# A two-layer encoder in one kernel: which engine forms the seven-product sums of the down-projection's weights, when a table slot is freed, and where four square sums and the norm factor stand

## The chip, the cores and the metric

The kernel runs on one core of one Trainium2 chip. The metric is the time of one execution in device microseconds (us), as the median of several executions. The core's engines each have their own list of instructions and run it in order: TensorE (PE in the profile; PEld is its weight load), VectorE (DVE), ScalarE (ACT), GpSimd (POOL), and SyncE (SP), whose list here holds nearly all loads from HBM.

## The reference, cut to what matters

One sequence of 512 tokens with 1024 features passes two layers, all in fp32. Each layer is an attention block and then an MLP; the change touches only the two MLPs.

```python
def rmsnorm(x, g):
    y = xf * lax.rsqrt(jnp.mean(xf * xf, axis=-1, keepdims=True) + EPS)
    return y * g

def sq_relu_mlp(h, w_up, w_down):          # w_up (1024, 4096), w_down (4096, 1024)
    u = jax.nn.relu(h @ w_up)
    return (u * u) @ w_down

for layer in range(2):
    ...
    h = h + sq_relu_mlp(rmsnorm(h, norm_ffn[layer]), ffn_w_up[layer], ffn_w_down[layer])
return rmsnorm(h, final_norm)
```

Below, `h @ w_up` is the MLP's first product and `(u * u) @ w_down` its second. "MLP0" and "MLP1" are the MLPs of the first and the second layer (`mlp(0)` and `mlp(1, last)` in the code).

## The kernel before

**Precision.** Every fp32 operand is split into a high part, which ScalarE rounds (`ACT.activation(hi, raw, Copy)`), and a low part, which VectorE forms as the rest (`raw - hi`). A product is then three matmuls: high by high, high by low, low by high. They are L607 to L609 with 512 columns, and L451 to L453 with 256 columns in the scheme below. The residual stream `hT` stays on the chip, transposed, in eight tiles of 128 by 512.

**Memory.** There are 32 slots of 128 x 1024 fp32 (`Slot`, `NSLOT`); `free` lists those not in use. Beside them stand rings: `raw` (four buffers for weights as loaded), `whi` (three) and `wlo` (four) for their parts.

**The seven-product scheme.** Most of both MLP products go through the class `Seven`: a block of 256 by 256 weights times two blocks of activations needs seven products of half-size blocks instead of eight, at the cost of sums of weight blocks before and sums of results after. One *chunk* is such a block of weights. `seven_chunk` makes one in three steps:

1. a load of 256 KB on SP into a `raw` buffer, or into a slot if more than `reserve[0]` slots are free;
2. three sums of weight blocks, L357, L358 and L359, on the engine `eng` (GpSimd when none is given);
3. the high part on ScalarE (L363), the low part on VectorE (L364). They write rings; a slot used for the raw weights is then given back.

`Seven.run` runs a *group*: a loop over the chunks (`kp`), and in it seven products (L451 to L453). At its end follows the evacuation: L459 on ScalarE, L460 to L463 on VectorE, and then `evac`, which in the second product of an MLP adds the result to `hT` on VectorE (L1579).

**Order of the weights.** `plan` lists the chunks in the order in which they will be used, and `weights(i)` runs ahead of use: the load is issued five chunks ahead (LOAD), and the sums directly with it in program order; high and low parts come two chunks ahead (AHEAD). Each engine's list is then what the scheduler of the framework makes of the program; what is wrapped in `keep_in_program_order` is fixed. `seven_chunk` fixes its sums on GpSimd, and lets the scheduler place sums on VectorE.

**The second product of an MLP** (`mlp`). `stage` computes the squared activations in two shares, and a first part of the second product runs between and after them. Then come four groups `m` = 0 to 3 of 256 output columns each, of eight chunks in MLP0 and seven in MLP1 (`SIZES`). During the groups, `beside(m, i)` is called at each product `i`; in MLP0 it splits the two halves of a last pair of raw activations, `V`, into high and low parts (`split`, L964), at `m == 1`. A short remaining product (`gens4`) uses them after the groups. Ahead of the groups, `reserve[0]` is 3.

**The table slot.** `bias_rows` builds the second layer's position-bias table in a slot `F`, and writes it out to HBM piece by piece by DMA; it runs in MLP0 beside the product ahead of the groups. The slot is kept as `hold["tables"]` and given back after the four groups.

**The planned engine.** `Seven.plan` gives VectorE the sums of chunk `kp == 3` (the fourth) in groups two to four (`c0` above 0, `pairs` given, that is only in the second products); all other chunks' sums are GpSimd's.

**The front of an MLP** (`first_product`). Eight tiles of `hT` are split (`split_g`), and their squares are formed on ScalarE (L621) and summed into `acc` (`sumsq_acc`, L623), all sums on VectorE. Matrix products on values not yet normalised begin at once (`plain`). Between two of them, `norm` computes the norm's factor: `compact_r` sums over partitions with TensorE (L628) and takes the inverse root with some small VectorE operations (L630, then L180 to L190); `bcast_cols` spreads it by four transposes on TensorE (L636), and ScalarE copies it to `rb` (L1368), which the evacuations of these products need. In MLP0 all this is called at product 11, in MLP1 at 13.

Of the kernel before, what the change touches and what calls it, by code (L numbers as in the profile page):

```python
# [30 lines left out]
def f32(ap):  # L31
    return ap.bitcast(F32)
# [3 lines left out]
def encoder_kernel(ctx: ExitStack, tc: tile.TileContext, ins, out, dbg=None):  # L36
    nc = tc.nc
    PE, ACT, DVE, POOL, SP = nc.tensor, nc.scalar, nc.vector, nc.gpsimd, nc.sync
# [37 lines left out]
    def bank(tag, bufs):  # L76
        return ps.tile([P, 512], F32, tag=tag, bufs=bufs, name=nm(tag))
# [4 lines left out]
    def sbk():  # L82
        return bank("s", 2)

    def stb():
        return bank("t", 2)

    def ob():
        return bank("o", 1)
# [180 lines left out]
    def plan(*spec, make=None):  # L270
        asked.append((make or chunk, spec))
        return len(asked) - 1
# [72 lines left out]
    reserve = [3]  # L345
# [23 lines left out]
    class Seven:  # L369
# [62 lines left out]

        def plan(self, w, c0, pairs=None):

            return [plan(w, pairs[kp] if pairs else 2 * kp, c0, DVE if pairs and c0 and kp == 3 else None,
                         make=seven_chunk)
                    for kp in range(self.np)]

# [131 lines left out]
    def tiles(c0, n):  # L570
        return [(c0 + o, min(P, n - o)) for o in range(0, n, P)]
# [46 lines left out]
    def sumsq_acc(k, acc, eng=None):  # L618

        sq = acc if k == 0 else scratch()  # L620
        ACT.activation(sq, hT[:, k, :], AF.Square)  # L621
        if k:
            (eng or POOL).tensor_tensor(acc, acc, sq, op=ALU.add)  # L623

    def compact_r(acc):
        b = stb()
        for i in range(4):
            PE.matmul(b[:, i : i + 1], acc[:, i * P : (i + 1) * P], ones[:, 0:1], start=True, stop=True)  # L628
        v = tiny(4)
        DVE.tensor_scalar(v, b[:, 0:4], 1.0 / D, EPS, op0=ALU.mult, op1=ALU.add)  # L630
        return rsqrt(v, 4)
# [8 lines left out]
    acc = pp.tile([P, S], F32, tag="p", name=nm("acc"))  # L640
# [150 lines left out]
    hold = {}  # L791
# [550 lines left out]
    def first_product(l):  # L1342

        w = ins["ffn_w_up"][l]
        X = [Slot() for _ in range(KD)]
        acc = pp.tile([P, S], F32, tag="p", name=nm("acc"))
        for k in range(KD):
            split_g(hT[:, k, :], gffn(l, k), X[k].pair())
            sumsq_acc(k, acc, DVE)
        xp = [s_.pair() for s_ in X]  # L1350
        U, R = [], []
        rb = keep([P, S], F32, "rb")
        state = dict(c=SIZES[l][0], ids=None, plain=False, split=iter(()), late=iter(()))
        x7 = Seven(KD)

        def ev(j, b):
            U.append(Slot())
            t = scratch()
            DVE.scalar_tensor_tensor(t, b, 0.0, rb, op0=ALU.max, op1=ALU.mult)
            uu = scratch()  # L1360
            ACT.activation(uu, t, AF.Square)
            split(uu, U[-1].pair())

        def norm():
            r = compact_r(acc)
            bk = stb()
            bcast_cols(lambda i: r[:, i : i + 1].to_broadcast([P, P]), P, bk)
            ACT.activation(rb, bk, AF.Copy)  # L1368

        def x_sums(kp):  # L1370
            raw = Slot(F32)
            for z in range(2):
                k = 2 * kp + z
                DVE.scalar_tensor_tensor(raw.t[:, S * z : S * z + S], hT[:, k, :], gffn(l, k), rb, op0=ALU.mult,
                                         op1=ALU.mult)
            for _ in x7.sums(kp, raw):
                pass

        held = tc.keep_in_program_order

        def finish(w_, to):

            held(ACT.activation(w_.t, w_.t, AF.Relu))
            held(ACT.activation(w_.t, w_.t, AF.Square))
            yield
            if to:
                for z, u in enumerate(to):
                    src, d = w_.t[:, S * z : S * z + S], u.pair()
                    held(ACT.activation(d[:, 0, :], src, AF.Copy))
                    held(DVE.tensor_tensor(d[:, 1, :], src, f32(d[:, 0, :]), op=ALU.subtract))  # L1390
                    if z == 0:
                        yield
                w_.free()
            yield

        def raw_evac(w_):
            R.append(w_)
            state["late"] = finish(w_, None)
            return True

        def pair_evac(w_):
            to = []
            for _ in range(2):

                left = state["n"] - len(U)
                to.append(Slot() if left > 3 or not state["halves"] else Halves(spare_p if left < 3 else spare_b))
                U.append(to[-1])
            state["late"] = finish(w_, to)
            return True

        def plain():
            four = product(w, 0, xp, tiles(0, 512), ev, lambda n: [mmb(), mmb(), mmb(), sbk()])
            two = product(w, 0, xp, tiles(512, 256), ev, lambda n: [sbk(), ob()], kstep=4)
            for n, _ in enumerate(four):
                if n == (11 if l == 0 else 13):
                    norm()
                if n == 14:
                    x_sums(0)
                    x_sums(1)
            for n, _ in enumerate(two):  # L1420
                if n == 4:
                    x_sums(2)
                if n == 6:
                    x_sums(3)
            flip[0] = 1
            for s_ in X:
                s_.free()
            state["plain"] = True

        def later(c, n):  # L1430

            for _ in state["split"] if (c, n) in ((0, 10), (0, 18), (1, 4)) else ():
                pass
            if (c, n) in ((0, 2), (0, 10), (0, 18), (1, 4)):
                state["split"] = x7.split({(0, 2): 0, (0, 10): 1, (0, 18): 2, (1, 4): 3}[c, n], tc.keep_in_program_order)
            next(state["split"], None)

        def ahead():
            state["ids"] = x7.plan(w, P * state["c"])

        def stage(n, raw=0, more=0):


            at = [], []
            if not state["plain"]:
                plain()
                at[0].extend(range(0, n, 2))
            nu, nr = (n - len(U)) // 2, raw // 2
            state["n"], state["halves"] = n, raw

            kinds = [1, 0] * nu if nr else [0] * nu
            kinds += [1] * (nr + nu - len(kinds)) + [1] * (more // 2)
            for i, kind in enumerate(kinds):
                ids = state["ids"]
                if i < nu + nr:
                    at[kind].append(state["c"])
                state["c"] += 2
                if i < len(kinds) - 1:
                    ahead()
                for u, _ in enumerate(x7.run(ids, (pair_evac, raw_evac)[kind])):  # L1460
                    if u in (14, 21, 24):
                        next(state["late"], None)
            if state["c"] == 32:
                x7.free()
            got = U[:n], R[: raw // 2], R[raw // 2 :], at, state["late"]
            U.clear()
            R.clear()
            return got

        return stage, ahead, later  # L1470
# [39 lines left out]
    def mlp(l, last=None):  # L1510
# [6 lines left out]
        w = ins["ffn_w_down"][l]  # L1517
        up4, gens4 = [], []

        def plain_last(k0, V):  # L1520
            left = list(V)
            gens4.extend(product(w, k0, up4, tiles(512 * c, 512), lambda j, b, c=c: ev(4 * c + j, b), nk=2 * len(V))
                         for c in range(2))

            def beside(m, i):
                if m == 1 and i % 8 == 4 and left:
                    w_ = left.pop(0)
                    for z in range(2):
                        U4.append(Slot())
                        up4.append(U4[-1].pair())  # L1530
                        split(w_.t[:, S * z : S * z + S], up4[-1])
                    w_.free()

            return beside
# [36 lines left out]
        for x in (work, bias):  # L1571
            for _ in x:
                pass
        reserve[0] = 3
        for m in range(4):

            def evac(w_):
                h2 = hT[:, 2 * m : 2 * m + 2, :]
                DVE.tensor_tensor(h2, h2, w_.t.rearrange("p (z n) -> p z n", z=2), op=ALU.add)  # L1579

            for i, _ in enumerate(u7.run(ids[m], evac)):
                beside(m, i)
        u7.free()
        if not last:
            hold["tables"].free()
        for gen in gens4:
            for _ in gen:
                pass
# [7 lines left out]
    acc = pp.tile([P, S], F32, tag="p", name=nm("acc"))  # L1596
# [481 lines left out]
```

## Time and profile before

| | before |
|---|---|
| median of three runs | 1160.11 us (1159.15 to 1160.34) |
| the profiled execution: its own time | 1159.6 us |
| the profiled execution: its span | 1157.8 us, mean granted clock 0.998 |
| ScalarE busy | 668.3 us (58%) |
| GpSimd busy | 591.3 us (51%) |
| moved by DMA | 134.37 MB, mean 116 GB/s |
| read from HBM | 110.61 MB |

The first row is the median over plain executions; the profile is of one further execution, so durations in the trace stand against that one's time. The span runs from the first instruction to the last. A "wait" in a view is idle time of an engine just ahead of an instruction, with the instruction on another engine, or the DMA, that ended it; "total, times, longest" stand behind it. In a timeline, a row has the start, the duration, the engine, the line, the operation, output and input by the names in the program, and in square brackets the idle time before it. Windows give, for a stretch of time, its length and then the busy time (with the number of instructions) of TensorE, its weight loads, VectorE, ScalarE and GpSimd in this order; the granted clock, the DMA share and GB/s follow.

The four groups of MLP0's second product begin at 494.42, 514.18, 534.20 and 555.53 us of the span, those of MLP1's at 1054.04, 1071.30, 1088.58 and 1106.85.

### The profile page before, as it was taken

How to read it: one execution, taken by the hardware profiler on the slowest of the kernel's cores; microseconds unless marked ns; L12 is line 12 of the kernel's file. 1: busy time of each engine (PE TensorE's matmuls, PEld its weight loads, DVE VectorE, ACT ScalarE, POOL GpSimd, SP SyncE). 2: the span in 40 equal slices, each digit the busy share in tenths (PEclk: the TensorE clock that was granted, in tenths of full speed). 3: DMA queues.
4: the chain of work that ended last, by engine and by line, in shares of the span. 5: the costliest groups of instructions: out<-in, count | busy, mean ns of one | idle time of the engine just before them, and what ended most of it. 6: DMA issues, size and time to landing. Idle time of an engine off the chain costs nothing.

```text
span 1157.8 us, 20539 instructions
## 1 busy us (share of the span) xinstructions
PE 1145.4 (99%) x7348; PEld 1022.4 (88%) x7348; DVE 896.9 (77%) x1562; ACT 668.3 (58%) x1135; POOL 591.3 (51%) x725
## 2 busy tenths in 40 slices
PE   9999999999999999999999999999999999999997
PEld 7787888888899999899988998988889999989995
DVE  6887988878867777967785666667996788697775
ACT  6676877755346668533354555545553666773445
POOL 4356252207688992378602232231387799436850
PEclk9999999999999999999999999999999999999999
DMA  7322414222523336923536574433344233372332
GB/s 236 105 75 70 99 55 137 65 67 97 167 81 98 86 92 157 257 92 101 157 98 164 144 180 128 117 108 119 103 152 127 74 92 92 79 188 71 119 119 73
DMA packets 115351, 134.37 MB, mean 116 GB/s; under 512 B 9796, under 2 KB 96753, under 8 KB 115249
## 3 DMA queue, kind: packets, MB, share of 16 engines
q1 hardware_dynamic: 110896, 120.09, 35.1%
q0 software_dynamic: 4032, 12.60, 5.4%
q8 instruction: 58, 0.95, 0.4%
q10 hardware_dynamic: 320, 0.36, 0.1%
q14 instruction: 45, 0.36, 0.1%
HBM read 110.61 MB, written 6.29 MB: 101 GB/s over the span
## 4 chain that ended last, share of the span: by engine, by line
PE 91%; DVE 3%; POOL 2%; DMA 1%; issue 1%; ACT 0%; DVEq 0%; POOLq 0%; ACTq 0%
PE mm L607 9%; PE mm L609 9%; PE mm L608 9%; PE mm L453 4%; PE mm L451 4%; PE mm L452 4%; PE s L1131 3%; PE t L451 3%; PE t L453 3%; PE t L452 3%; PE o L1119 3%; PE s L609 2%; PE s L608 2%; PE s L607 2%; PE t L1106 2%; PE s L451 2%
## 5 line engine op out<-in xcount | busy, mean ns | idle before, releaser
L607 PE MATMUL mm<-a,whi 128*128 128x512 f32 x428 | 173.6, 406 | 0.2
L364 DVE TENSOR_TENSOR wlo<-a,whi 128x896 fp32r<-128x896 f32 x103 | 126.1, 1227 | 57.5 <-ACT whi L363 56.8
L609 PE MATMUL mm<-a,wlo 128*128 128x512 f32 x428 | 169.0, 396 | 0.0
L608 PE MATMUL mm<-a,whi 128*128 128x512 f32 x428 | 168.9, 395 | 0.0
L363 ACT ACTIVATE whi<-a 128x896 fp32r<-128x896 f32 x103 | 97.8, 949 | 108.1 <-PE s L452 24.4
L233 ACT ACTIVATE whi<-raw 128x1024 fp32r<-128x1024 f32 (+3 forms) x100 | 92.2, 924 | 68.4 <-PE s L608 24.4
L223 DVE TENSOR_TENSOR wlo<-raw,whi 128x1024 fp32r<-128x1024 f32 (+4 forms) x97 | 110.0, 1139 | 26.7 <-ACT whi L233 26.4
L453 PE MATMUL mm<-a,wlo 128*128 128x256 f32 x430 | 120.7, 281 | 0.2
L451 PE MATMUL mm<-a,whi 128*128 128x256 f32 x430 | 120.7, 281 | 0.0
L452 PE MATMUL mm<-a,whi 128*128 128x256 f32 x430 | 120.3, 280 | 0.0
L363 ACT ACTIVATE whi<-raw 128x896 fp32r<-128x896 f32 x61 | 57.7, 952 | 84.4 <-POOL raw L359 44.6
L364 DVE TENSOR_TENSOR wlo<-raw,whi 128x896 fp32r<-128x896 f32 x61 | 73.7, 1222 | 35.9 <-ACT whi L363 35.8
L359 POOL TENSOR_TENSOR a<-a 128x128 f32<-128x128 f32 x103 | 95.3, 926 | 8.1
L358 POOL TENSOR_TENSOR a<-a 128x256 f32<-128x256 f32 x103 | 93.1, 904 | 8.1
L609 PEld LDWEIGHTS mm<-a,wlo 128*128 128x128 f32 x428 | 80.3, 188 | 18.1
L607 PEld LDWEIGHTS mm<-a,whi 128*128 128x128 f32 x428 | 80.5, 188 | 17.2 <-issue 0.8
L608 PEld LDWEIGHTS mm<-a,whi 128*128 128x128 f32 x428 | 80.7, 189 | 14.9 <-DVE a L964 0.2
L1139 POOL TENSOR_SCALAR p<-p,ti 128x512 f32<-128x512 f32 x64 | 45.2, 707 | 85.9 <-DVE ti L1138 61.3
L1721 POOL TENSOR_SCALAR p<-p,ti 128x256 f32<-128x256 f32 x64 | 35.3, 563 | 104.5 <-DVE ti L1720 91.4
L451 PE MATMUL t<-a,whi 128*128 128x256 f32 x312 | 87.6, 281 | 0.0
L453 PE MATMUL t<-a,wlo 128*128 128x256 f32 x312 | 87.3, 280 | 0.0
L452 PE MATMUL t<-a,whi 128*128 128x256 f32 x312 | 87.3, 280 | 0.0
(432 smaller groups left out, 3587.9 us busy)
## 6 DMA issues: line engine op xcount, KB each, us to landing
a<-in_ffn_w_up_dram SPq DMA_DIRECT2D x102, 256.0 KB, 2.8
raw<-in_ffn_w_down_dram SPq DMA_DIRECT2D x34, 512.0 KB, 4.5
raw<-in_ffn_w_down_dram SPq DMA_DIRECT2D x59, 256.0 KB, 2.7
raw<-in_od_w_qkv_dram SPq DMA_DIRECT2D x64, 128.0 KB, 3.0
raw<-in_ffn_w_up_dram SPq DMA_DIRECT2D x12, 512.0 KB, 3.9
wlo<-in_ffn_w_down_dram POOLq DMA_DIRECT2D x12, 512.0 KB, 6.3
a<-a SPq DMA_DIRECT2D x18, 256.0 KB, 3.3
bx<-a SPq DMA_DIRECT2D x32, 128.0 KB, 5.4
```

The lines of the kernel that those rows point to most:

```text
L223: z = lambda: (eng or DVE).tensor_tensor(to, src, f32(high), op=ALU.subtract)
L233: ACT.activation(hi[:, 0:m], raw[:, 0:m], AF.Copy)
L358: held(eng.tensor_tensor(r[:, 4:6], r[:, 2:3].to_broadcast([P, 2, P]), r[:, 0:7:6], op=ALU.add))
L359: held(eng.tensor_tensor(r[:, 7], r[:, 3], r[:, 5], op=ALU.subtract))
L363: ACT.activation(hi[:, 0:896], raw[:, 128:1024], AF.Copy)
L364: DVE.tensor_tensor(lo[:, 0:896], raw[:, 128:1024], f32(hi[:, 0:896]), op=ALU.subtract)
L451: PE.matmul(o, wh, x[:, 0], start=kp == 0 and n in (0, 1, 3, 5), stop=False, skip_group_check=True)
L452: PE.matmul(o, wh, x[:, 1], start=False, stop=False, skip_group_check=True)
L453: PE.matmul(o, wl, x[:, 0], start=False, stop=kp == self.np - 1, skip_group_check=True)
L607: PE.matmul(o, wh, xh, start=first, stop=False)
L608: PE.matmul(o, wh, xl, start=False, stop=False)
L609: PE.matmul(o, wl, xh, start=False, stop=last)
```

## The change

It has five parts:

- *Sums:* in groups two to four of both second products, the chunks `kp` 2 and 5 (the third and the sixth) have their sums on VectorE, in place of chunk 3 (the fourth).
- *Slots:* in MLP0, the table slot is given back before the second group (`m == 1`) and not after the fourth, and `reserve[0]` is 2 during the groups. So more raw weights may be loaded into slots in place of `raw` buffers. MLP1 keeps 3, and has no table.
- *Split of the last raw pair* (`beside`): in MLP0 at `m == 2` instead of `m == 1`.
- *Square sums:* in MLP0, the sums of squares of tiles 1 to 4 go to GpSimd; tiles 5 to 7, and all of MLP1, stay on VectorE. Tile 0 has none.
- *Norm:* `norm` becomes a generator of two steps. In MLP0 the factor is computed at product 8 and spread at product 12 (both were at 11); in MLP1 both stay at 13.

```diff
@@ Seven.plan
-            return [plan(w, pairs[kp] if pairs else 2 * kp, c0, DVE if pairs and c0 and kp == 3 else None,
+            return [plan(w, pairs[kp] if pairs else 2 * kp, c0, DVE if pairs and c0 and kp in (2, 5) else None,
                          make=seven_chunk)
                     for kp in range(self.np)]
@@ first_product
         for k in range(KD):
             split_g(hT[:, k, :], gffn(l, k), X[k].pair())
-            sumsq_acc(k, acc, DVE)
+            sumsq_acc(k, acc, DVE if l or k > 4 else POOL)
...
         def norm():
             r = compact_r(acc)
+            yield
             bk = stb()
             bcast_cols(lambda i: r[:, i : i + 1].to_broadcast([P, P]), P, bk)
             ACT.activation(rb, bk, AF.Copy)
+            yield
...
+            factor = norm()
             for n, _ in enumerate(four):
-                if n == (11 if l == 0 else 13):
-                    norm()
+                for _ in range(((8, 12), (13, 13))[l].count(n)):
+                    next(factor)
@@ mlp, beside
-                if m == 1 and i % 8 == 4 and left:
+                if m == 2 and i % 8 == 4 and left:
@@ mlp
-        reserve[0] = 3
+        reserve[0] = 3 if last else 2
         for m in range(4):
+            if m == 1 and not last:
+                hold["tables"].free()
...
             for i, _ in enumerate(u7.run(ids[m], evac)):
                 beside(m, i)
         u7.free()
-        if not last:
-            hold["tables"].free()
```

## Prediction

> **What bounds the kernel now.** First the page's head, then the waits of the matrix engine's weight loader, which stands ahead of each matmul and so shows a late operand first.
>
> ```profile
> span 1157.8 us, 20539 instructions
> PE 1145.4 (99%) x7348; PEld 1022.4 (88%) x7348; DVE 896.9 (77%) x1562; ACT 668.3 (58%) x1135; POOL 591.3 (51%) x725
> ...
> PEld s L453 <- DVE wlo L364: 1.4, 1, 1.4
> ...
> PEld mm L453 <- DVE wlo L364: 0.8, 3, 0.3
> ...
> PEld t L636 <- DVE ti L190: 0.7, 1, 0.7
> ```
>
> TensorE has something to do for 99% of the span, and the change takes no matmul away. So it can only gain what TensorE waits for. The waits are "total, times, longest". L453 is the third matmul of a product of Seven.run, the one that needs the low weight part made at L364. It waits 1.4 us once and 0.8 us in three further cases, 2.2 us in all. L636, the broadcast of the first MLP's norm factor, waits 0.7 us. These two places are what the change can reach.
>
> The timelines of TensorE and VectorE show the large wait. Chunks of a group are counted from one; eight make a group in the first MLP.
>
> ```profile
> 534.20 0.28 PE L451 MATMUL s<-a,whi 128*128 128x256 f32 x1
> ...
> 541.65 0.28 PE L451 MATMUL s<-a,whi 128*128 128x256 f32 x1
> 541.77 0.28 PE L452 MATMUL s<-a,whi 128*128 128x256 f32 x1
> 543.29 0.38 PE L453 MATMUL s<-a,wlo 128*128 128x256 f32 x1 [1.24 <-DVE wlo L364]
> ```
>
> ```profile
> 532.79 1.16 DVE L364 TENSOR_TENSOR wlo<-raw,whi 128x896 fp32r<-128x896 f32 x1 [2.69 <-ACT whi L363]
> 533.88 0.55 DVE L357 TENSOR_TENSOR raw<-raw 128x128 f32<-128x128 f32 x1
> 534.46 0.57 DVE L358 TENSOR_TENSOR raw<-raw 128x256 f32<-128x256 f32 x1
> 535.06 0.72 DVE L359 TENSOR_TENSOR raw<-raw 128x128 f32<-128x128 f32 x1
> 535.70 1.08 DVE L364 TENSOR_TENSOR wlo<-raw,whi 128x896 fp32r<-128x896 f32 x1
> ...
> 538.12 1.17 DVE L364 TENSOR_TENSOR wlo<-raw,whi 128x896 fp32r<-128x896 f32 x1
> 539.20 0.41 DVE L462 TENSOR_TENSOR a<-a,mm 128x256 f32<-128x256 f32 x1
> 539.72 0.69 DVE L463 TENSOR_TENSOR a<-a,s 128x512 f32<-128x512 f32 x1
> 540.44 1.53 DVE L1579 TENSOR_TENSOR hT<-hT,a 128x1024 f32<-128x1024 f32 x1
> 541.90 3.61 DVE L364 TENSOR_TENSOR wlo<-raw,whi 128x896 fp32r<-128x896 f32 x3
> ```
>
> Group three begins at 534.20 (call a group's start T). Its fourth chunk begins 7.45 us later and needs its low part 0.24 us after that, at T+7.69. VectorE, in order, has in front of it the fourth chunk's own sums (533.88 to 535.70, 1.82 us), two low parts, and the whole evacuation of the group before (L460 and L461, which stand between the two low parts at 535.70 and 538.12 and are left out above, then L462, L463, and L1579, which adds the result to the residual hT). It starts that low part at 541.90. TensorE goes on at 543.29, 1.40 us after its beat of 0.12. Why VectorE was that late shows in the chain of waits, beside the median of all such loads (last column), and on GpSimd:
>
> ```profile
> 524.34 4.53 DMA raw<-in_ffn_w_down_dram
> ...
> 539.31 4.65 DMA raw<-in_ffn_w_down_dram
> ```
>
> ```profile
> raw<-in_ffn_w_down_dram SPq DMA_DIRECT2D x59, 256.0 KB, 2.7
> ```
>
> ```profile
> 531.32 0.46 POOL L359 TENSOR_TENSOR raw<-raw 128x128 f32<-128x128 f32 x1
> 531.73 0.46 POOL L357 TENSOR_TENSOR raw<-raw 128x128 f32<-128x128 f32 x1
> 532.27 0.74 POOL L358 TENSOR_TENSOR raw<-raw 128x256 f32<-128x256 f32 x1
> 533.08 1.19 POOL L359 TENSOR_TENSOR raw<-raw 128x128 f32<-128x128 f32 x1
> ```
>
> A chunk's load waits for the low part four chunks earlier (four raw buffers). The load at 524.34 took 4.53 instead of 2.7, and GpSimd then needs 2.54 us a chunk (531.73 to 533.08 + 1.19), as long as TensorE (7.45/3 = 2.48). So a load once late is not caught up.
>
> **The change, part by part.** *Slots for raw weights, first MLP.* In the changed program's order three loads go to slots: chunk six of group two, two and six of group three. The slot's data need no raw buffer, so the loads after them start one or two chunks (2.5 to 5 us) earlier. It adds no DMA. The first of the three now stands in SP's queue ahead of the loads from chunk six of group one on, which wait for low parts anyway. Cost nothing; cover is that wait.
>
> *Sums on VectorE.* Chunks three and six of groups two to four in both MLPs go to VectorE, chunk four goes back to GpSimd: 18 more instructions on VectorE. A chunk's three sums cost VectorE 1.82 us here and 1.26 us in the next rows (1106.31 to 1107.57), and they take 2.54 us off GpSimd.
>
> ```profile
> 1106.31 0.29 DVE L357 TENSOR_TENSOR raw<-raw 128x128 f32<-128x128 f32 x1 [2.19 <-DMA raw<-in_ffn_w_down_dram]
> ...
> 1107.57 1.08 DVE L364 TENSOR_TENSOR wlo<-raw,whi 128x896 fp32r<-128x896 f32 x1
> ```
>
> ```profile
> 534.00:554.00 20.00, 18.76 (x160) 18.55 (x159) 14.70 (x16) 7.79 (x9) 17.08 (x22) 1.00 0.35 106
> ```
>
> In this stretch of about a group VectorE is busy 14.70 of 20 and GpSimd 17.08 (third and fifth figure behind the length). One chunk more makes VectorE some 16.5, one fewer makes GpSimd some 14.5. Neither becomes the bound by its total; what counts is the order within VectorE's list. The third chunk's high part cannot begin before T+0.13 (ScalarE's buffer comes free with the group before, see the next row against the third chunk's start 560.47) and takes 0.96, so its low part begins at T+1.1.
>
> ```profile
> 560.60 0.96 ACT L363 ACTIVATE whi<-raw 128x896 fp32r<-128x896 f32 x1 [1.51 <-PE s L452]
> ```
>
> By starts in the fence above: low part 1.08, L462 0.52, L463 0.72, L1579 1.46, low part 1.20 (3.61/3).
> - Group two: 1.1+1.08+0.52+0.72+1.46+1.20 = T+6.08 against T+7.69. Its wait ends.
> - Group three: L1579 now stands behind the fourth low part: T+4.62, 3.1 us to spare. The last split of the raw pair, moved here from group two (two L964), fits into that. The 1.4 us end.
> - Group four, and groups two to four of the second MLP: the sixth chunk's sums stand *inside* the evacuation, between L462, L463, L1579 and the fourth low part. T+6.08 plus 1.26 to 1.82 is T+7.34 to T+7.90: no wait up to 0.2 us. But VectorE also waits there for that chunk's load. The load follows the low part of the group's second chunk, which ends at about T-0.3 (one chunk before T, and 0.13+0.96+1.08). It lands at T+2.4 at 2.7 us; the sum's turn comes at T+2.7. With 4.65 it lands at T+4.35, 1.65 us late: a wait of 1.3 to 1.9 us. Behind VectorE's wait stand L463, L1579 and the low part, and behind that TensorE.
>
> In the window shown, two loads in some twenty were that slow, and at 1106.31 VectorE waited 2.19 us for just such a load. That one of four places is hit I take as one in two: 0.8 us for all four, bounds 0 and 4 x 1.9 = 7.6. Sums that stand ahead of the seventh chunk's low part can wait for a load too, but that low part is due two chunks (5 us) later: nothing up to a slow load.
>
> The row of GpSimd's L359 is 0.46 alone and 1.19 beside VectorE's low part of 532.79 to 533.95, ending 0.32 behind it: the two exclude each other. [...]
>
> *Front of the first MLP.* Four square sums go to GpSimd, the factor is computed three products earlier, 2.07 us by the 0.69 that the kernel's planner puts on one (MM3).
>
> ```profile
> POOL 4356252207688992378602232231387799436850
> ...
> L623 DVE TENSOR_TENSOR acc<-acc,sc x21: 677/686/694, 244.1 to 818.3; 128x512 f32<-128x512 f32 x21
> L664 POOL TENSOR_TENSOR acc<-acc,sc x5: 1293/1303/1638, 11.7 to 20.2; 128x512 f32<-128x512 f32 x5
> ...
> 257.09 0.68 DVE L623 TENSOR_TENSOR acc<-acc,sc 128x512 f32<-128x512 f32 x1
> ...
> 259.99 1.22 DVE L223 TENSOR_TENSOR wlo<-raw,whi 128x1024 fp32r<-128x1024 f32 x1 [1.07 <-ACT whi L233]
> 262.61 0.16 DVE L630 TENSOR_SCALAR ti<-t 128x4 f32<-128x4 f32 x1 [1.40 <-PE t L628]
> 262.81 0.17 DVE L180 TENSOR_SCALAR ti<-ti 128x4 int32<-128x4 int32 x1
> ...
> 265.01 0.16 DVE L190 SCALAR_TENSOR_TENSOR ti<-ti,ti 128x4 f32<-128x4 f32 x1
> ```
>
> ```profile
> 261.63 0.95 PE L628 MATMUL t<-ones,acc 128*128 128x1 f32 x8
> ...
> 265.23 0.65 PE L636 MATMUL t<-cst,ti 128*128 128x128 f32 x4 [0.23 <-DVE ti L190]
> ```
>
> L628 would come at 261.63 - 2.07 = 259.56. The sum is ready at 257.77 now, 1.8 us sooner; a GpSimd add is at most 0.95 longer (1.638 against 0.686), and GpSimd is idle there: in the slices of the page, 28.9 us each, the ninth, 231.6 to 260.5, shows a 0. In the new order the low part of 259.99 falls between L630 and L180: L628 + 0.98 + 0.08 + 1.14, then 2.36 to the end of L190, is 4.6. L636 stands 5/3 of a product (0.70) later behind L628 than now: 265.23 - 261.63 + 0.70 = 4.3. The wait, 0.39 on TensorE by its beat, becomes about 0.3: a gain of 0.1, bounds -0.2 and 0.4.
>
> **Sum.** The execution's own time is 1159.6, 0.5 under the median 1160.11. 1159.6 - 2.2 - 0.1 + 0.8 = 1158.1; on the median's footing 1158.6.
>
> **Rivals.**
> - *No load is late.* For it: the median 2.7, loads that start earlier. Against it: the two slow loads. 1159.6 - 2.2 - 0.4 = 1157.0, so 1157.5.
> - *The sums inside the evacuation take the place of the old wait (slower).* Place: VectorE between L462 and the fourth low part, four times. Price 1.3 to 1.9 each, mean 1.6: 1160.1 - 2.3 + 6.4 = 1164.2. It decides from 1.15 us each on (4.6 in all). For it: only 0.3 us of margin on the load, and the 2.19 us row. Against it: most loads are at 2.7.
> - *No relief.* VectorE and GpSimd exclude each other, or the slots bring no load forward, and the same 2.2 us return elsewhere: 1160.1. For it: L359's 1.19. Against it: a chunk's sums take VectorE 0.7 to 1.3 us less than GpSimd, and group three's list loses 3 us ahead of the due point.
>
> **Numbers.** Forecast (gain 0.6 to 2.3) 0.48, no late load 0.20, slower 0.17, no relief 0.15. 0.2% is 2.3 us, about what a measurement of this kernel can tell from no change, and as much as all the waits in reach. Faster by more (under 1157.8): 0.15 of no late load, whose 1157.5 is only just beyond, and 0.05 of the forecast's low end, 0.20. Slower by more: the slower rival's 0.17 and 0.03 of no relief, 0.20. Same 0.60. The forecast's own range is 1157.8 to 1159.5; the range given, 1157.0 to 1162.0, takes in no late load (1157.5 less 0.5 for the spread of the runs) and no relief, and of the slower rival the part up to four waits of 1.05 (1160.1 - 2.3 + 4.2), and leaves out the rest of it.
>
> **What would show it.** Right: no L453 wait in groups two and three of the first MLP; waits of at most one or two L453 in group four or the second MLP, each with VectorE's L357 idle for a DMA inside the evacuation; L636 waiting about as long as now. Wrong: the 1.4 us still at the fourth chunk of group three; L628 waiting for acc; L453 waits of over 1 us in three or four of the four groups; or a wait at the seventh chunk.

## The result, and the profile after

| | before | changed |
|---|---|---|
| median of 14 runs each | 1159.97 us (1159.15 to 1160.64) | 1157.50 us (1156.85 to 1158.44) |
| ratio to before | | 0.998 (95%: 0.9971 to 0.9988) |
| the profiled execution: its own time, span | 1159.6, 1157.8 us | 1158.44, 1156.7 us |

The kernel became 2.47 us faster, 0.21%: just beyond the 0.2% that the prediction took as the border of "no change", with an interval (0.12% to 0.29%) that lies on both sides of it. By that border the case "faster", to which the prediction gave 0.20, came, and not "same" (0.60). The profiled execution of the changed kernel is the slowest of its 14; its group one begins at 495.56, 1.1 us later than before's 494.42, although nothing ahead of the first MLP's front was changed. Two rows of the waits of TensorE (total, times, longest), both from the first 12 us, show where most of that is from:

```profile
PEld t L646 <- issue: 1.4, 2, 1.2
...
PE t L646 <- DVE hT L657: 0.8, 1, 0.8
```

So stages are compared here by their own length, not by their place in the span. In the waits between 490 and 576 us, which hold the four groups of the first MLP, TensorE has no row left (before: 1.9 us on L453). Windows of these stretches (length, then TensorE, its loads, VectorE, ScalarE and GpSimd) show it busy throughout, where before it was busy 18.76 of 20:

```profile
534.00:554.00 20.00, 20.00 (x172) 20.00 (x171) 16.89 (x20) 8.96 (x11) 14.66 (x19) 1.00 0.30 93
```

VectorE's timeline at group three, the place of the old 1.40 us:

```profile
537.70 1.17 DVE L364 TENSOR_TENSOR wlo<-raw,whi 128x896 fp32r<-128x896 f32 x1
538.79 0.41 DVE L462 TENSOR_TENSOR a<-a,mm 128x256 f32<-128x256 f32 x1
539.30 0.69 DVE L463 TENSOR_TENSOR a<-a,s 128x512 f32<-128x512 f32 x1
539.91 1.08 DVE L364 TENSOR_TENSOR wlo<-raw,whi 128x896 fp32r<-128x896 f32 x1
540.91 1.22 DVE L1584 TENSOR_TENSOR hT<-hT,a 128x1024 f32<-128x1024 f32 x1
```

The group begins at 535.08, so the fourth low part starts at T+4.83 and ends at T+5.91 (before: T+7.70 and T+9.04), and the addition to hT (L1579 before, L1584 now) stands behind it. Group four, where the sixth chunk's sums stand inside the evacuation:

```profile
556.10 1.48 DVE L364 TENSOR_TENSOR wlo<-raw,whi 128x896 fp32r<-128x896 f32 x1
557.51 0.41 DVE L462 TENSOR_TENSOR a<-a,t 128x256 f32<-128x256 f32 x1
557.84 0.28 DVE L357 TENSOR_TENSOR raw<-raw 128x128 f32<-128x128 f32 x1
558.04 0.67 DVE L463 TENSOR_TENSOR a<-a,o 128x512 f32<-128x512 f32 x1
558.64 0.41 DVE L358 TENSOR_TENSOR raw<-raw 128x256 f32<-128x256 f32 x1
558.98 1.21 DVE L1584 TENSOR_TENSOR hT<-hT,a 128x1024 f32<-128x1024 f32 x1
560.11 0.28 DVE L359 TENSOR_TENSOR raw<-raw 128x128 f32<-128x128 f32 x1
560.32 2.35 DVE L364 TENSOR_TENSOR wlo<-raw,whi 128x896 fp32r<-128x896 f32 x2
```

L357 shows no idle time: its load had landed. From the starts, the three sums take 0.20 + 0.34 + 0.21 = 0.75 us here. T is 554.84 (first matmul of the group), so the fourth low part starts at T+5.48 and ends at T+6.55; it is due at T+7.63. In the second MLP no L453 wait is left either. The front, on TensorE and on VectorE:

```profile
261.04 0.95 PE L628 MATMUL t<-ones,acc 128*128 128x1 f32 x8
...
265.44 0.65 PE L636 MATMUL t<-cst,ti 128*128 128x128 f32 x4
```

```profile
259.34 0.68 DVE L623 TENSOR_TENSOR acc<-acc,sc 128x512 f32<-128x512 f32 x1
...
265.22 0.16 DVE L190 SCALAR_TENSOR_TENSOR ti<-ti,ti 128x4 f32<-128x4 f32 x1
```

The sum of squares ends 1.0 us ahead of L628, the factor at 265.38, just ahead of L636 at 265.44. L636 comes 0.27 us behind the matmul ahead of it, where the beat is 0.23: of its 0.39 us almost nothing is left.

### The profile page after: what moved, and what is told of

It reads as the page before. It is cut to its first block, busy times and chain, and to the rows that moved or that the text cites. A ratio compares the mean times of both kernels' runs of the same rounds, so it can differ in the third digit from the quotient of the medians.

```text
span 1156.7 us, 20518 instructions
## 1 busy us (share of the span) xinstructions
PE 1144.4 (99%) x7348; PEld 1022.1 (88%) x7348; DVE 905.6 (78%) x1576; ACT 668.7 (58%) x1135; POOL 579.5 (50%) x711
## 4 chain that ended last, share of the span: by engine, by line
PE 94%; DVE 2%; DMA 1%; issue 1%; ACT 1%; SPq 0%; POOL 0%; DVEq 0%; ACTq 0%; POOLq 0%
PE mm L607 8%; PE mm L608 8%; PE mm L609 8%; PE mm L451 4%; PE mm L453 4%; PE mm L452 4%; PE t L451 3%; PE t L453 3%; PE t L452 3%; PE s L1131 3%; PE o L1119 3%; PE s L451 2%; PE s L453 2%; PE s L609 2%; PE s L452 2%; PE s L607 2%
## 5 line engine op out<-in xcount | busy, mean ns | idle before, releaser
L364 DVE TENSOR_TENSOR wlo<-a,whi 128x896 fp32r<-128x896 f32 x106 | 131.9, 1248 | 56.1 <-ACT whi L363 55.5
L609 PE MATMUL mm<-a,wlo 128*128 128x512 f32 x428 | 168.9, 396 | 0.0
L363 ACT ACTIVATE whi<-a 128x896 fp32r<-128x896 f32 x106 | 100.6, 949 | 110.7 <-PE s L452 30.3
L453 PE MATMUL mm<-a,wlo 128*128 128x256 f32 x430 | 120.3, 280 | 0.0
L359 POOL TENSOR_TENSOR a<-a 128x128 f32<-128x128 f32 x104 | 98.6, 948 | 8.2
L363 ACT ACTIVATE whi<-raw 128x896 fp32r<-128x896 f32 x58 | 55.1, 953 | 81.0 <-PE s L452 24.6
L609 PEld LDWEIGHTS mm<-a,wlo 128*128 128x128 f32 x428 | 80.2, 188 | 18.3
L364 DVE TENSOR_TENSOR wlo<-raw,whi 128x896 fp32r<-128x896 f32 x58 | 70.8, 1230 | 26.2 <-ACT whi L363 26.1
L453 PE MATMUL t<-a,wlo 128*128 128x256 f32 x312 | 87.2, 280 | 0.0
```

Source lines behind the costliest of these rows:

```text
L359: held(eng.tensor_tensor(r[:, 7], r[:, 3], r[:, 5], op=ALU.subtract))
L363: ACT.activation(hi[:, 0:896], raw[:, 128:1024], AF.Copy)
L364: DVE.tensor_tensor(lo[:, 0:896], raw[:, 128:1024], f32(hi[:, 0:896]), op=ALU.subtract)
L453: PE.matmul(o, wl, x[:, 0], start=False, stop=kp == self.np - 1, skip_group_check=True)
L609: PE.matmul(o, wl, xh, start=False, stop=last)
```

## The experiments

Twelve kernels, each with 11 runs beside 33 of the kernel before on the same chip. "Difference" is median less before's median there. Most intervals are about 1 us to either side, so a single part of under 1 us is not resolved by its time alone; there the trace has to speak.

| run | median | before | difference | ratio, 95% interval |
|---|---|---|---|---|
| sums | 1159.18 | 1159.95 | -0.77 | 0.9985 to 1.0002 |
| slots_split | 1158.96 | 1159.95 | -0.99 | 0.998 to 0.9998 |
| front_only | 1160.01 | 1159.95 | +0.06 | 0.9992 to 1.001 |
| no_front | 1158.10 | 1159.95 | -1.85 | 0.9976 to 0.9993 |
| no_slots | 1157.96 | 1159.59 | -1.63 | 0.9981 to 0.9998 |
| third_only | 1158.03 | 1159.59 | -1.56 | 0.9978 to 0.9995 |
| no_squares | 1157.28 | 1159.59 | -2.31 | 0.9973 to 0.9991 |
| more_slots | 1160.95 | 1159.59 | +1.36 | 1.0002 to 1.002 |
| add_later | 1158.75 | 1159.48 | -0.73 | 0.9984 to 1.0002 |
| add_later_all | 1160.44 | 1159.48 | +0.96 | 0.9999 to 1.0017 |
| fetch_earlier | 1157.43 | 1159.48 | -2.05 | 0.9974 to 0.9991 |
| fetch_later | 1160.29 | 1159.48 | +0.81 | 1.0001 to 1.0019 |

The two theories in the expectations: by "list", TensorE waited because of what stands ahead of the fourth low part in VectorE's own order; by "loads", because raw weights were loaded too late.

### Parts alone

**sums**

```diff
-            ... DVE if pairs and c0 and kp == 3 else None
+            ... DVE if pairs and c0 and kp in (2, 5) else None
```

> The kernel before with one part of the change: the sums of the third and sixth chunk on VectorE in place of the fourth's, in both MLPs. If VectorE's list ahead of the fourth low part made the old wait (theory 'list'), the 1.4 us at group three go and the 0.2 us in the second MLP too: about 1158.3. If loads that start late made it (theory 'loads'), nothing is gained here, for the raw buffers are as before: 1159.9; and where the sums inside the evacuation wait for a late load, it is 1.3 us or more slower: 1161.

-0.77: between the two. In the profiled execution the waits of group three and of the second MLP's L453 are gone, as "list" says. At group three the addition (L1579) still stands *ahead* of the fourth low part here:

```profile
539.24 1.21 DVE L1579 TENSOR_TENSOR hT<-hT,a 128x1024 f32<-128x1024 f32 x1
540.38 0.55 DVE L359 TENSOR_TENSOR raw<-raw 128x128 f32<-128x128 f32 x1
540.85 3.90 DVE L364 TENSOR_TENSOR wlo<-raw,whi 128x896 fp32r<-128x896 f32 x3
```

The group begins at 534.48, so this low part starts at T+6.37 and ends at T+7.44, 0.20 us ahead of its due time. A load came late ahead of this group too (4.21 us, issued at 525.38). So that the fourth chunk's sums left the list was enough in this trace, and in that of no_slots below; the addition did not have to move.

A new wait of 2.03 us beyond the beat stands in group four. The chain of waits (start, length, what) and VectorE's timeline there:

```profile
554.79 4.69 DMA raw<-in_ffn_w_down_dram
```

```profile
557.20 0.40 DVE L462 TENSOR_TENSOR a<-a,t 128x256 f32<-128x256 f32 x1
559.50 0.29 DVE L357 TENSOR_TENSOR raw<-raw 128x128 f32<-128x128 f32 x1 [1.90 <-DMA raw<-in_ffn_w_down_dram]
559.71 0.68 DVE L463 TENSOR_TENSOR a<-a,o 128x512 f32<-128x512 f32 x1
...
562.78 3.34 DVE L364 TENSOR_TENSOR wlo<-raw,whi 128x896 fp32r<-128x896 f32 x3
```

This is the prediction's slower rival, in its place and at about its price (2.03 against 1.3 to 1.9 there): a load of 4.69 us, VectorE idle for 1.90 inside the evacuation, L463, L1579 and the low part late behind it. That profiled execution is the slowest of its 11 (1160.79), so it shows what the wait is, not how often it comes.

**slots_split**

```diff
+        reserve[0] = 3 if last else 2
+            if m == 1 and not last: hold["tables"].free()
-                if m == 1 and i % 8 == 4 and left:
+                if m == 2 and i % 8 == 4 and left:
```

> The kernel before with two parts: the table slot freed after group one with two slots in reserve, and the split of the last raw pair in group three; sums on the engines as before. Theory 'loads': the 1.4 us at group three go, the second MLP's 0.2 stays: about 1158.5. Theory 'list': the fourth chunk's own sums still stand ahead of the evacuation, so 0.7 to 1.4 us stay: 1159.2 to 1160.

-0.99, between the two again. The trace tells more. VectorE at group three and at group four of this kernel (the addition is L1581 here):

```profile
539.03 0.69 DVE L463 TENSOR_TENSOR a<-a,s 128x512 f32<-128x512 f32 x1
539.64 1.47 DVE L364 TENSOR_TENSOR wlo<-raw,whi 128x896 fp32r<-128x896 f32 x1
541.03 1.48 DVE L1581 TENSOR_TENSOR hT<-hT,a 128x1024 f32<-128x1024 f32 x1
...
559.10 0.69 DVE L463 TENSOR_TENSOR a<-a,o 128x512 f32<-128x512 f32 x1
559.83 1.78 DVE L1581 TENSOR_TENSOR hT<-hT,a 128x1024 f32<-128x1024 f32 x1
561.52 4.15 DVE L364 TENSOR_TENSOR wlo<-raw,whi 128x896 fp32r<-128x896 f32 x3
```

With the split of the raw pair in group three, the scheduler puts the addition *behind* the fourth low part there, and TensorE doesn't wait. In group four it stands ahead, and TensorE waits 0.85 us beyond its beat. The order is not all that differs: the fourth chunk's own sums are done 2.6 us before group three begins, and 0.6 us after group four begins. Had the addition (1.4 us) stood ahead in group three too, that low part would have ended, by these rows, some 0.1 to 0.2 us past its due time. So this run does not tell the two theories apart: the chunk that was loaded earlier takes most of the wait away, the order the rest.

**front_only**

```diff
+            sumsq_acc(k, acc, DVE if l or k > 4 else POOL)
+                for _ in range(((8, 12), (13, 13))[l].count(n)): next(factor)
```

> The kernel before with the front alone: four square sums on GpSimd, factor at product 8, spread at product 12. The 0.39 us ahead of L636 go, nothing else changes: 1159.6. If the wait returns at L628 or L636, 1160.0.

+0.06: inconclusive in time. In the trace the 0.39 us ahead of L636 are gone, as expected, and TensorE waits 0.88 in group three (before: 1.40). It also waits 0.68 us at 621 us, in the second layer's attention, where the profiled execution of before doesn't wait; those of ten other kernels here do, the changed one among them.

### Parts undone

**no_front** (the changed kernel with the front as before)

> The changed kernel with the front of the first MLP as before (square sums on VectorE, norm at product 11). If the parts add up, 0.4 us slower than the changed kernel: 1157.9. If the front carries none of it, 1157.5.

-1.85, 0.6 less than the changed kernel's -2.47, where 0.4 was expected. L636 waits 0.39 again, and group four has 0.42 by a load of 3.92 us: VectorE's L357 waits 0.75 for it.

**no_slots** (the changed kernel with the table slot and the reserve as before)

> The changed kernel without the slots: table slot freed after the groups and three slots in reserve, as before; sums, split of the last pair and front as changed. If the slots are what keeps the sums inside the evacuation from waiting for late loads, a wait of 0.5 to 2 us stands in group four and perhaps in group two or three: 1158.5 to 1159. If the slots carry nothing, 1157.5.

-1.63; 0.8 less than the whole, with overlapping intervals. Its profiled execution has one wait of 0.30 us in group four, with VectorE waiting for no load inside that evacuation. The slots do bring loads forward: counted from the start of group one, the last eight weight loads of the first MLP's groups are issued 0.1 to 3.8 us earlier in the changed kernel than here. That this is worth time is likely, not shown.

**third_only**

```diff
-            ... kp in (2, 5) else None
+            ... kp in (2,) else None
```

> The changed kernel with VectorE's sums for the third chunk alone; the sixth chunk's go back to GpSimd, so that no sum stands inside the evacuation. If those sums are the weak place, no wait is left in group four: 1157.2 to 1157.5. If GpSimd then falls behind by its 2.54 us a chunk, high parts wait for GpSimd and 0.5 to 1.4 us come back: 1158 to 1159.

-1.56, on the second expectation's side: TensorE waits 0.75 us in group four, with no load late. GpSimd has no gap there from 549 to 562 us, a chunk takes it 2.51 us (553.07 to 555.58 in its timeline), and the evacuation begins 1.9 us after T, where in the changed kernel it begins 0.1 us before T:

```profile
553.07 0.46 POOL L357 TENSOR_TENSOR raw<-raw 128x128 f32<-128x128 f32 x1
553.61 0.74 POOL L358 TENSOR_TENSOR raw<-raw 128x256 f32<-128x256 f32 x1
554.42 1.19 POOL L359 TENSOR_TENSOR raw<-raw 128x128 f32<-128x128 f32 x1
555.58 0.46 POOL L357 TENSOR_TENSOR raw<-raw 128x128 f32<-128x128 f32 x1
```

So by this trace the sixth chunk's sums belong on VectorE because GpSimd, at TensorE's own pace of 2.47 us a chunk, cannot catch up. In time the two kernels are 0.9 us apart, with overlapping intervals.

**no_squares** (the changed kernel with all square sums on VectorE)

> The changed kernel with all square sums of the first MLP on VectorE, as before; the norm still in two steps at products 8 and 12. If the move to GpSimd is needed for the earlier factor, L628 or L636 waits 0.3 to 0.6 us: 1158.0. If the two steps alone do it, 1157.5 and no wait at either.

-2.31, as good as the whole. L636 waits 0.27 us in its trace; the sum of squares is ready 1.8 us ahead of L628 (L623 ends at 258.51, L628 at 260.29), earlier than with four adds on GpSimd (1.0 ahead). So the move isn't needed for the sum, and the time doesn't resolve it. But 0.27 of the 0.39 us stay without it, for another reason: from the start of L180 to the end of the last L190, VectorE's steps of the inverse root take 2.36 or 2.37 us in all seven traces of this case with the sums on VectorE, and 2.14 or 2.15 in all seven with four of them on GpSimd. Why they are shorter there stayed open.

### The order alone

**add_later**

```diff
+                (evac keeps the addition for later, unless m == 3)
+            for i, _ in enumerate(u7.run(ids[m], evac)):
+                if i == 7 and late_add: tc.keep_in_program_order(late_add.pop(0)())
```

and the fourth chunk's low part is fixed in that order too, so that it comes first.

> The kernel before with one change of order alone: in both second products, the addition of a group's result to hT stands behind the low part of the next group's fourth chunk, not ahead of it (and the last raw pair is split one chunk later). No sums, slots or norm moved. Theory 'list': the list ahead of the fourth low part is 1.2 to 1.5 us shorter, so the waits at group three (1.4 us) and the small ones go, and only the 0.4 us of the front stay: 1158.0. Theory 'loads': nothing is loaded earlier, 1159.5 or more.

The trace does what "list" says: TensorE has no wait in the four groups of the first MLP, with sums, slots and loads as before.

```profile
540.49 0.69 DVE L465 TENSOR_TENSOR a<-a,s 128x512 f32<-128x512 f32 x1
541.09 1.46 DVE L364 TENSOR_TENSOR wlo<-raw,whi 128x896 fp32r<-128x896 f32 x1
542.48 1.48 DVE L1583 TENSOR_TENSOR hT<-hT,a 128x1024 f32<-128x1024 f32 x1
```

(L465 and L1583 are L463 and L1579 of before.) The fourth chunk's first matmul comes at 543.38, so its third is due at 543.62; with the addition ahead, the low part would have ended at some 544.0. All loads issued from 530 us on landed within 2.82 us in this execution, so it doesn't show the order against late loads. The time misses 1158.0 by 0.75. In the profiled execution, the slowest of its 11, a wait takes the place of the old ones in the second MLP, where the final transposes read hT; it may be the reason:

```profile
PEld mm L1971 <- DVE hT L1583: 1.1, 1, 1.1
```

How much of the 1.40 us is order alone, the kernel before shows in its other groups. In group four the list is the same, but the loads issued from 544 us on landed in 2.6 to 3.3 us:

```profile
554.06 0.29 DVE L357 TENSOR_TENSOR raw<-raw 128x128 f32<-128x128 f32 x1 [0.22 <-DMA raw<-in_ffn_w_down_dram]
...
560.38 1.77 DVE L1579 TENSOR_TENSOR hT<-hT,a 128x1024 f32<-128x1024 f32 x1
562.07 4.16 DVE L364 TENSOR_TENSOR wlo<-raw,whi 128x896 fp32r<-128x896 f32 x3
```

The fourth chunk's sums begin at T-1.47 there (group three: T-0.32), and TensorE waits 0.31 us; in group two they begin at T-1.09, and it waits 0.14. So the list alone costs 0.1 to 0.3 us, and some 1.1 of the 1.40 come from the late load.

**add_later_all** (the same edit in the changed kernel)

> The changed kernel with the same change of order. If waits behind sums inside the evacuation still cost it something in some executions, they have 1.2 us more room: 1157.0 to 1157.3, and no L453 waits in any group. If the changed kernel has none left, 1157.5.

A miss: +0.96, 3.4 us behind the changed kernel's -2.47. The kept results hold a slot longer, fewer raw weights go to slots, and the scheduler puts the sixth chunk's sums and the evacuation's last two operations (L462 and L463 in the changed kernel) ahead of the *third* low part of group three, which stands ahead of both there and starts at 538.15 here; TensorE waits 1.04 us for it, and 0.84 us at the transposes of the second MLP. These two come to 1.9 us, against the 3.4. The profiled execution is the fastest of its 11 (1158.79, 1.65 under their median), so the rest stayed open.

**more_slots**

```diff
-        reserve[0] = 3 if last else 2
+        reserve[0] = 2 if last else 1
```

> The changed kernel with one slot less in reserve in both MLPs (1 and 2), so that the sixth chunk's raw weights, in group four of the first MLP and in groups of the second, go to slots too and are loaded earlier. If late loads inside the evacuation still cost the changed kernel something in some executions, they go: 1157.0 to 1157.3, no VectorE L357 waiting for a DMA by over 0.5 us there. If they cost nothing, 1157.5.

A miss, and the clearest run. More loads went to slots, and it lost 3.8 us against the changed kernel. VectorE and TensorE at group three:

```profile
540.19 0.55 DVE L359 TENSOR_TENSOR a<-a 128x128 f32<-128x128 f32 x1
540.66 1.82 DVE L964 TENSOR_TENSOR a<-a,a 128x512 fp32r<-128x512 f32 x2
542.40 2.34 DVE L364 TENSOR_TENSOR wlo<-raw,whi 128x896 fp32r<-128x896 f32 x2
```

```profile
543.80 0.39 PE L453 MATMUL s<-a,wlo 128*128 128x256 f32 x1 [2.14 <-DVE wlo L364]
...
545.37 0.41 PE L452 MATMUL t<-a,whi 128*128 128x256 f32 x1
545.58 0.41 PE L453 MATMUL t<-a,wlo 128*128 128x256 f32 x1
```

```profile
534.00:554.00 20.00, 17.86 (x139) 17.66 (x138) 15.89 (x21) 7.55 (x9) 13.43 (x18) 0.91 0.24 74
```

The scheduler put both halves of the raw pair's split (L964), the sixth chunk's sums and the addition ahead of the fourth low part: TensorE waits 2.30 us beyond its beat. And from 1.2 us after the wait its matmuls follow each other at 0.21 us instead of 0.12 for 3.4 us; the granted clock is 0.50 from 545.0 to 548.3, and 0.91 over the 20 us. The wait and the slow stretch together cost 3.9: group three takes 23.71 us here and 19.76 in the changed kernel.

### What makes a load late

The trace also has DMA transfers of instructions. On one queue ("q8 instruction" on the page: 58 packets, 0.95 MB, 16 KB each; one for each 253 matmuls and weight loads of TensorE, 7348 of each in all, so they are taken here for TensorE's), they come 13.6 to 16.8 us apart in the first MLP's groups of the kernel before. They were compared with the 256 KB loads of raw weights in the groups of both MLPs, over all 14 traces of this case (673 loads):

```
transfer of 16 KB begins, after the load's issue   loads   median us to landing   over 3.3 us
0.0 to 0.5 us                                        16            3.02                1
0.5 to 1.0 us                                        24            3.58               20
1.0 to 1.5 us                                        17            4.34               17
1.5 to 2.6 us                                        59            2.75               14
none in that time                                   557            2.62               18
```

Without a transfer, 18 of 557 loads were late too, and what decides between 1.5 and 2.6 us stayed open. Two runs moved these transfers against the work, by the number of idle products that TensorE does in its first 10 us.

**fetch_earlier** (`idle_work(3)` becomes `idle_work(8)`, in the changed kernel)

> The changed kernel with five more idle products on TensorE in its first 10 us (they compute nothing that is used), which moves each of TensorE's 16 KB instruction transfers some 1.2 us earlier against the work. If these transfers make loads late, the load that is issued at the start of group four of the first MLP takes over 4 us in place of 2.8, VectorE's L357 waits over 1 us for it inside the evacuation and TensorE 1 to 2 us: 1158.5 to 1160.5, up to 1 us of it for the added products. If late loads have nothing to do with them, no such wait and 1157.5 to 1158.5.

The transfer moved, by 1.7 us instead of 1.2: from T+2.05 to T+0.33 in group four. That is 0.36 us after the load, too early for the late landings of the table, and the load took 2.98 us; no wait there, and -2.05 for the time. The expectation for this place failed. In the same execution, the slowest of its 11, two other loads, issued at 508.50 and 524.93, had a transfer 1.17 and 1.25 us behind them and took 4.26 and 4.49 us; TensorE waited 0.86 us at the fourth chunk of group two and 1.01 at its seventh. VectorE's wait for the second load:

```profile
529.52 0.29 DVE L357 TENSOR_TENSOR raw<-raw 128x128 f32<-128x128 f32 x1 [3.35 <-DMA raw<-in_ffn_w_down_dram]
```

**fetch_later** (the run "sums" with `idle_work(8)` as 3 and `idle_work(3)` as 0)

> The kernel before with the sums moved (the run 'sums'), and with eight idle products fewer at the start, which moves TensorE's instruction transfers some 1.9 us later against the work. If they made the load of 4.69 us in group four, it lands in under 3 us, the 2.03 us wait there goes, and the time is 1157.3 to 1158.3. If not, 1159.2 as in 'sums'.

In the trace as expected: the transfer comes 1.97 us after the load of group four (in "sums" 1.04), the load lands in 2.62 instead of 4.69, and the wait of 2.03 is 0.24. The time isn't: +0.81, 1.6 behind "sums", where 1 to 2 us less were expected. TensorE's start costs part of it (group one begins at 496.15 instead of 494.96), and other loads meet a transfer instead (4.25 us for the one issued at 497.60, 4.67 at 1058.40), so the run ties the late load to the transfer in one place and says nothing on its price in time.

## Why the prediction was right, step by step

- *Only what TensorE waits for can be gained.* Right: by its beat, the waits of before that are gone in the trace are 0.39 (L636, but for 0.04), 1.85 in the first MLP's groups and 0.23 in the second's, 2.47 together; the medians differ by 2.47, within an interval of about 1 us to either side. That the two figures are equal is luck: the changed kernel's profiled execution has waits that before's has not (0.6 us on L1131, 0.4 on L1720, 0.3 on L609), in places that the change doesn't touch, and its time is only 1.16 under that of before's.
- *The 1.40 us at group three end, since the addition to hT moves behind the fourth low part.* The wait ended, and the addition does stand behind. But the sum for it was off: T+4.62 is where the low part was to end, and it ended at T+5.91, 1.7 us ahead of its due time instead of 3.1. The third low part was to begin at T+1.1 and began at T+2.62, since half of the raw pair's split (L964, 1.17 us) stands in the evacuation ahead of it. For group two the same sum was right: T+6.08 forecast, T+6.01 measured. Nor is the addition's place the whole cause. In "sums" and no_slots the wait goes with the addition still ahead, because the fourth chunk's sums have left the list; in add_later it goes with those sums in place, because the addition is behind. By these traces the 1.40 took all three together, the sums, the addition and the late load; no run shows the addition's place alone against a late load.
- *The sums inside the evacuation.* The place of a late load was right, and its price nearly (sums: 1.90 idle, 2.03 lost, against 1.3 to 1.9). Two sizes were off. The three sums take 0.75 us there, not 1.26 to 1.82, and the fourth low part ends at T+6.55 instead of T+7.34 to 7.90. In the rows used for the price the three sums follow one another directly, each beginning after the one before has ended, and GpSimd works beside all (1.82) or the last (1.26) of them; here another instruction stands behind each and begins before the sum's end, and GpSimd is idle from 557.91 to 560.33. And the 0.8 us that the sum held for such waits (one of four places hit in one execution of two) was too much: the changed kernel's profiled execution has none, and its median is near the sum without them. How often they come is not shown: kernels with the same sums have such waits of 2.03 (sums) and 0.42 us (no_front), and fetch_earlier has 0.86 and 1.01 by late loads ahead of the fourth and of the seventh chunk of group two.
- *So the likeliest case was not the one that came.* The forecast 1158.6 was 1.1 above the result; the rival "no late load", 1157.5, is what came. The step that failed is the term of 0.8 us for late loads; that they are possible was right.
- *The front.* Forecast 0.1 (bounds -0.2 to 0.4); the trace gained 0.35. L636 came 4.40 behind L628 (forecast 4.3), the factor was ready 4.34 behind it (forecast 4.6), 0.06 ahead of L636. Without square sums on GpSimd (no_squares) it is ready at 4.57, as forecast. The move to GpSimd delays the sum, as the prediction allowed (by 0.8 us, against at most 0.95), and the sum still comes in time. What the prediction missed is that the steps of the inverse root become 0.2 us shorter with it.
- *Slots cost nothing and bring loads forward.* Three loads go to slots, as forecast (issued at 490.94, 520.10 and 525.14), and later ones start up to 3.8 us earlier than in no_slots (forecast 2.5 to 5). They cost nothing in the changed kernel. As more_slots shows, that isn't a property of slots: with one more, the scheduler's order changed and 3.8 us were lost.
- *No relief because VectorE and GpSimd exclude each other.* It didn't come. What the trace of before shows is narrower: each of GpSimd's 77 L359 that begin under a low part of VectorE ends 0.32 us behind it (1.19 to 1.37 long), while the five that begin under L461 or L463 take 0.46, as alone. Work moved between the two engines did help here: a chunk's sums cost VectorE 0.75 us against GpSimd's 2.51, and third_only, which moves one chunk back to GpSimd, has 0.75 us of wait again.

## What to carry to other kernels

Where an engine stands ahead of the bottleneck's operand, read its list in order: what counts is which instructions stand ahead of the due one, and when the first of them could begin, not how busy the engine is; 20 us with 16.89 on VectorE had no wait, 20 us with 14.70 had 1.4. An edit that only frees memory or moves a split can change that order through the scheduler (more_slots, add_later_all lost 3.4 to 3.8 us against the changed kernel), so the order is to be compared after each edit. The price of a late transfer belongs into the forecast as a case with its chance, not as a mean in the likeliest sum.

## What the hardware showed that was not expected

- *A 256 KB weight load landed late where a 16 KB transfer of TensorE's instructions began 0.5 to 1.5 us after its issue*: over 3.3 us in 37 of 41 cases, and 3.84 to 4.88 in all 17 with 1.0 to 1.5 us between; with none in its time, 2.62 in the median. Another count of TensorE's instructions moved the transfers: 1.7 us earlier in fetch_earlier, where the loads of 4.26 and 4.49 us have one 1.17 and 1.25 us behind their issue; in fetch_later from 1.04 to 1.97 us behind the issue of group four's load, which landed in 2.62 instead of 4.69.
- *After a wait of 2.3 us TensorE ran at nearly half its pace for 3.4 us* (more_slots: 0.21 instead of 0.12 a matmul, granted clock 0.50). After one of 2.03 us (sums) the granted clock is 1.00 over the 20 us from 554 us on. It was seen in one execution; that the wait brought the clock down is not shown.
